# An encoder trunk on one core: how many weight quarters the first chunks hold, and in what order their first sums are made

## The chip, the cores and the metric

The kernel runs on one core of one Trainium2 chip. A core has five engines that work side by side, each on its own queue in program order: TensorE (PE, matrix products, with its weight loads shown apart as PEld), VectorE (DVE), ScalarE (ACT), GpSimd (POOL) and SyncE (SP, which here only issues transfers). The metric is the device time of one execution in microseconds (us), smaller being better. Three runs of the kernel before took 955.87, 958.1 and 958.0 us, so the median is 958.0 us.

## The reference

A two-layer encoder trunk over 512 tokens of width 1024. Each layer normalises the tokens, projects them with one wide matrix, mixes them (layer 0 by dilated sliding-window attention, layer 1 by grouped-query attention with a rotary over a grid), lets four memory heads look at 256 memory tokens, gates the heads, and projects the result back onto the residual.

```python
for i in range(DEPTH):
    h = rmsnorm(x, norm_g[i])
    mem_h = rmsnorm(mem, mem_norm_g[i])
    if i % 2 == 0:
        proj = jnp.einsum('bsd,de->bse', h, w_in_a[j])
        ...
        o_mix = mixer_dilated(qkv, qn_a[j], kn_a[j], ang_a)
    else:
        proj = jnp.einsum('bsd,de->bse', h, w_in_b[j])
        ...
    o_mem = memory_attention(q_mem, mem_h, w_mem_kv[i], mem_qn_g[i], mem_kn_g[i])
    y = jnp.concatenate([o_mix, o_mem], axis=-1) * jax.nn.silu(gate)
    x = x + jnp.einsum('bse,ed->bsd', y, w_out[i])
```

All of it is in 32-bit floats. The memory attention normalises the keys of each head (`k = rmsnorm(kv[:, :, 0], kn_g)`) before they meet the queries.

## The kernel before, in words

**Products.** Every number is kept as a high part (rounded to the matrix engine's 32-bit format) and a low part (what the rounding left). A product is made of three: high by high (line 173), low activation by high weight (174), high activation by low weight (177). ACT makes the high part of a weight tile (`wh`, line 309) and DVE the low part (`wo`, line 319).

**Seven products in place of eight.** A wide projection is cut into quarters, and the classic scheme of seven block products is used: the activations are needed as the quarters 12, 11, 22 and the sums S1, S2, S3, S4, the weights as the quarters 21, 11, 22 and the sums T1, T2, T3, T4. The order of the products is 12, 11, S1, S2, S4, S3, 22 with the weights 21, 11, T1, T2, 22, T3, T4.

**Chunks and groups.** The weights are read in chunks. In the order of work these are chunk 1 and 2 (keys and values of the memory, four groups each), chunk 0 (a value projection, two tiles of each weight, so fourteen groups), chunk 3 (memory queries, seven groups), chunk 4 (the first head, fourteen groups), and so on. A group is the set of matrix products made with one or two weight tiles. Groups are counted from 0 here: chunk 1 is groups 0 to 3, chunk 2 is 4 to 7, chunk 0 is 8 to 21, chunk 3 is 22 to 28.

**What orders the work.** The order is written by a small planner when the program is made. After every group it calls `advance`, which in this order writes low parts, at most one weight sum, up to two high parts, and then loads (`dma`, line 260, on the SP queue). Then it steps a counter of slots: slot n comes behind group n-1. Routines that are waiting for their slot (`spawn` with a delay, `yield n`) go on then. Work put in with `late` stands at the end of a slot, with `soon` at the start of the next. All engines keep this order; they wait for each other only for data and for room.

**Weight sums.** T1 is made by DVE (line 278). T2 (line 283), T3 (288) and T4 (293) are made by transfers issued on the POOL queue that add one tile, or a tile in DRAM, onto another. T2 needs T1, and T4 needs T2 and the low part of 21. A sum is only looked at when its load is two groups old, and T1 of the kernel before not ahead of group 8 (`T1_AT`).

**Loads.** `KEEP` is the number of weight tiles that may be loaded and not used up at a time, by the kind of chunk: 8 for chunks 1 and 2, 10 for chunk 0, 9 for chunks 3 and 4. The tiles (512 KB, name `wl`) share 23 buffers with the input rows and the activations. Stores of results (line 1062, `v0d`) and the small loads of `setup` (lines 975 to 978) stand in the same SP queue.

**The tokens.** Four blocks of 128 tokens are normalised one slot after the other from slot 2 on (`prep`): `norm_1` squares and sums on ACT, `norm_2` scales on DVE (line 495), `first_t` turns blocks 0 and 1 with the matrix engine, giving the quarters 12 and 11. `diffs_t` turns blocks 2 and 3 and makes S1 and S3 on DVE (561, 562), with a high and a low part for S1 (161, 164). `rest_t` makes S2 and S4 (573, 575) and the parts of S2, S4, S3 and 22 (569, 570), two slots between them.

**Memory keys.** `mem_kv` normalises the keys, turns them on the matrix engine (line 606, into a PSUM tile), writes the high part on ACT (643) and the low part on DVE (646). The turned keys and the turned tokens (name `xT`, line 501) take their PSUM tiles from the same four banks (`at`), the products (`pj`) from four others. The planner hands out, of the free banks, the one that has been free longest, and a bank is free when the last instruction that reads its tile has been written into the order.

Of the kernel before, what the change touches and what calls it, by code (L numbers as in the profile page):

```python
# [21 lines left out]
TCKW = {}  # L22
NBIG, NM4, NS2, SCRATCH = 7, 23, 14, 2048
RING, LEAD = 4, 2
BULK, ACTIVE, SET_AT, T1_AT, MEM_B, PREP_Y, PREP_B, HALF, SET_B = 2, 2, 15, 8, 14, 1, 1, {"a": 3, "b": 3, "o": 0}, 9
MEM_STEP = 1, 1
MEM_D = 4
DIRECT, DIRECT_B = (7,), (4, 5, 6, 7)
LO_K, LO_V = (0, 5), (0, 3)
PD = 2  # L30
EO = 2, 2, 1, 2, 2, 1
YB = {"m": (2, 2), "k": (1, 1, 1), 0: (1, 2, 1), 1: (1, 2, 1)}
# [6 lines left out]
SEQ = [1, 2, 0] + list(range(3, len(PLAN)))  # L39
T4_AT = {4: 4}  # L40
T1_DMA = 17
KEEP = {"T2": 8, "T2b": 6, "O1": 6, "W1": 9, "W2": 10, "W2s": 9, "W1bs": 9, "W1b": 7, "W2b": 9}


# [84 lines left out]
def trunk_kernel(ctx: ExitStack, tc: tile.TileContext, x, mem, wall, norm_g, mem_norm_g, gcol,  # L129
# [9 lines left out]
    drv = Driver()  # L139
# [4 lines left out]
    def m4(dt=F32, name="m4"):  # L144
        return pool.tile([128, 1024], dt, tag="m4", name=name, bufs=NM4)

    def s2(dt=F32, name="s2"):
        return pool.tile([128, 512], dt, tag="s2", name=name, bufs=NS2)
# [7 lines left out]
    def sm(n, name):  # L156
        return small.tile([128, n], F32, tag="sm%d" % n, name=name)
# [35 lines left out]
    class Weights:  # L193
        def __init__(self):
            self.items, self.last, self.need, self.allocs, self.sums = [], [], [], [], []
            self.users, self.kinds = {}, []
            g = 0
            for c in SEQ:
                kind, d = PLAN[c], sum(pieces(k) for k in PLAN[:c])
                base = len(self.items)  # L200
                if kind in GROUPS:
# [20 lines left out]
                else:  # L222
# [3 lines left out]
                    for k in ORDER:  # L226
                        for x in range(n):
# [5 lines left out]
                            if k != "T4":  # L233
                                self.users[c, k, x] = 1 if k in ("22", "T3") or k == "11" and c >= T1_DMA else 2
                            g += 1
                self.kinds += [kind] * (g - len(self.kinds))
            assert sum(pieces(k) for k in PLAN) == wall.shape[0]
            self.g = -1
            self.live = 0
# [9 lines left out]
                self.live -= 1  # L249

        def dma(self, most=9):
            while self.allocs and self.live < KEEP[self.allocs[0][2]] and most:
                most -= 1
                key, d, _ = self.allocs.pop(0)
                self.live += 1
                self.tile[key] = m4(name="wl")
                self.load_at[key] = self.g
                if key[1][0] != "T":
                    self.at[key] = self.g
                nc.sync.dma_start(self.tile[key], wall[d])  # L260
# [4 lines left out]
        def sum(self, force=False, want=None):  # L265

            for n, (key, d) in enumerate(self.sums[:8]):
                if want and key != want:
                    continue
                c, k, x = key  # L270
                if k == "T1" and c >= T1_DMA:
                    if not self.ripe(self.load_at, key, force):
                        continue
                    G.dma_start(self.tile[key], wall[d], accum_op=ALU.add)
                elif k == "T1":
                    if not (self.ripe(self.load_at, key, force) and self.ripe(self.at, (c, "11", x), force)) or self.g < T1_AT and not force:
                        continue
                    V.tensor_tensor(self.tile[key], self.tile[key], self.tile[c, "11", x], ALU.add)
                    self.use((c, "11", x))
                elif k == "T2":  # L280
                    if not (self.ripe(self.load_at, key, force) and self.ripe(self.at, (c, "T1", x), force, 1 if c < T1_DMA else None)):
                        continue
                    G.dma_start(self.tile[key], self.tile[c, "T1", x], accum_op=ALU.add)  # L283
                    self.use((c, "T1", x))
                elif k == "T3":
                    if not self.ripe(self.load_at, key, force):
                        continue
                    G.dma_start(self.tile[key], wall[d], accum_op=ALU.add)
                else:
                    if not (self.ripe(self.lo_at, (c, "21", x), force, 1) and self.ripe(self.at, (c, "T2", x), force, T4_AT.get(c))):  # L290
                        continue
                    self.tile[key] = self.tile[c, "21", x]
                    G.dma_start(self.tile[key], self.tile[c, "T2", x], accum_op=ALU.add)  # L293
                    self.use((c, "T2", x))
                self.at[key] = self.g
                self.sums.pop(n)
                return True
            return False

        def hi(self, force=False):  # L300
            i = self.n_hi
            if i >= len(self.items) or not self.ripe(self.at, self.items[i], force, 1 if self.items[i][1] == "T1" and self.items[i][0] < T1_DMA else None):
                return False
# [140 lines left out]
    def rstd_of(ss, n):  # L444

        r = sm(n, "rstd")
        e = sm(n, "mse")
        G.tensor_scalar(e, ss, EPS, None, ALU.add)  # L448
        G.tensor_tensor(r, e, half[:, 0:n], ALU.pow)  # L449
        return r  # L450
# [29 lines left out]
    def norm_1(xb, both=False):  # L480

        ss = sm(2, "ss")
        for j in range(2):
            jk = s2(name="sq")
            if both and j:
                V.tensor_tensor_reduce(jk, xb[j], xb[j], 1.0 / 1024.0, 0.0, ALU.mult, ALU.add, ss[:, j:j + 1])
            else:
                A.activation(jk, xb[j], AF.Square, scale=1.0 / 32.0, accum_out=ss[:, j:j + 1])
        r, e = sm(1, "rstd"), sm(1, "mse")
        G.tensor_tensor(e, ss[:, 0:1], ss[:, 1:2], ALU.add)  # L490
        return rstd_of(e, 1)

    def norm_2(xb, r, row, js=(0, 1)):
        for j in js:
            V.scalar_tensor_tensor(xb[j], xb[j], r, row[j], ALU.mult, ALU.mult)
# [44 lines left out]
    def slot(H, k, c):  # L540
        if c == 0:
            part[k] = big(F32R, "h" + k).rearrange("p (a k t) -> p a k t", a=2, k=4)
        else:
            H[k] = part[k]
        cs = slice(c * 128, (c + 1) * 128)
        return part[k][:, 0, :, cs], part[k][:, 1, :, cs]

    def first_t(H, top, c):

        ps = [(k, turn4(top[j], *slot(H, k, c))) for k, j in (("12", 1), ("11", 0))]  # L550
        for k, p in ps:
            A.copy(whole(k, c), p)

    def diffs_t(H, low, c):

        f22 = whole("22", c)
        A.copy(f22, turn4(low[1], None, None))
        p = turn4(low[0], None, None)
        yield 1
        s1, s3 = whole("S1", c), whole("S3", c)  # L560
        V.tensor_tensor(s1, p, f22, ALU.subtract)
        V.tensor_tensor(s3, full["11", c], p, ALU.subtract)
        split(*slot(H, "S1", c), s1)

    def rest_t(H, c, ds, spread=False):

        def put(k, f):
            hi, lo = slot(H, k, c)
            A.copy(hi, f)
            drv.late(lambda: V.tensor_tensor(lo, f, hi.bitcast(F32), ALU.subtract))  # L570

        s1, s2_, s4, s3, f22 = [full.pop((k, c)) for k in ("S1", "11", "12", "S3", "22")]
        V.tensor_tensor(s2_, s1, s2_, ALU.subtract)
        if not spread:
            V.tensor_tensor(s4, s4, s2_, ALU.add)
        put("S2", s2_)
        if spread:
            yield ds[0] - 1
            V.tensor_tensor(s4, s4, s2_, ALU.add)
            yield 1  # L580
        else:
            yield ds[0]
        put("S4", s4)
        yield ds[1]
        put("S3", s3)
        yield ds[2]
        put("22", f22)
        yield 1
# [24 lines left out]
    def halves(t):  # L613
        return [t[:, 0:512], t[:, 512:1024]]
# [339 lines left out]
    H, H2 = {}, {}  # L954
    xb = [halves(t) for t in xt]

    def prep():

        n = {}
        for c in range(5):  # L960
            if c < 4:
                n[c] = norm_1(xb[c])
            if c:
                norm_2(xb[c - 1], n[c - 1], rows["x"])
            if 1 < c < 4:
                first_t(H, xb[c - 2], c - 2)
            yield 1
        for c in range(2):
            yield from diffs_t(H, xb[2 + c], c)
            drv.spawn(rest_t(H, c, (2, 2, 2)), 1)  # L970
            yield 1

    def setup():

# [68 lines left out]
    def ahead(u, b):  # L1043
# [5 lines left out]
        if (u, b) == (0, 1):  # L1049
            place_m(0, 1)  # L1050
            place_m(1, 1)

    drv.spawn(prep(), PD)
    drv.spawn(setup(), SET_AT)

# [605 lines left out]
```

## Time and profile before

One execution was profiled. It took 955.29 us, of which 953.4 us lie between its first and last instruction (the span).

| | before |
|---|---|
| median of three runs | 958.0 us |
| profiled execution / its span | 955.29 / 953.4 us |
| PE busy | 939.3 us |
| DVE busy | 790.3 us |
| ACT busy | 680.8 us |
| POOL busy | 336.0 us |
| weight tiles loaded on the SP queue | 222 of 512 KB |

The profile gives, for each engine, busy time, the idle time ahead of an instruction and the one that ended it; the chain of waits that ends with the last instruction; and the timeline of each queue. Times in a timeline are counted from the start of the span. In a row of the timeline the columns are the start, the time from the first start to the last end, the engine, the line of the code, the operation, the tile that is written and those that are read, the shape, the number of instructions put together, and in brackets the idle time before them with what ended it. SPq is the SP queue's issuing of transfers.

### The profile page before, as it was taken

To read this page: it belongs to the slowest core of one execution; us is meant where nothing else is said; L and a number is where in the kernel's file an instruction comes from. 1 tells how busy PE (TensorE), PEld (TensorE's weight loads), DVE (VectorE), ACT (ScalarE), POOL (GpSimd) and SP (SyncE) were. 2 spreads that over 40 slices of the span, in tenths; PEclk is the share of its full clock that TensorE was granted. 3 is DMA by queue.
4 is the path that set the end of the run, shared out by engine and by line. 5 is a ranking of instruction groups with operands and counts; after the bars stand their busy time and mean duration, and the time that the engine had idled before them with its cause. 6 is when DMAs were issued, how large, how long until landed. Compare 5 with 4: busy or idle time off the path is not lost.

```text
span 953.4 us, 16569 instructions
## 1 busy us (share of the span) xinstructions
PE 939.3 (99%) x5680; PEld 832.2 (87%) x5680; DVE 790.3 (83%) x1409; ACT 680.8 (71%) x1700; POOL 336.0 (35%) x484
## 2 busy tenths in 40 slices
PE   8999999999999999999999999999899999999998
PEld 6878888888888888888889998888899999998886
DVE  6878776878888888979788999877988898779982
ACT  7773789686868686767775768547778877878860
POOL 3312423557454546463836111213232330111110
PEclk9999999999999999999999999999999999999999
DMA  9699966869787869696877989979966687786524
GB/s 352 271 217 337 335 156 177 289 123 265 148 259 157 264 155 265 155 257 142 229 182 197 259 200 252 288 251 314 240 158 132 192 236 174 210 210 178 123 59 129
DMA packets 86198, 203.51 MB, mean 213 GB/s; under 512 B 25057, under 2 KB 34529, under 8 KB 86114
## 3 DMA queue, kind: packets, MB, share of 16 engines
q1 hardware_dynamic: 66962, 139.46, 42.8%
q0 software_dynamic: 17856, 60.83, 34.4%
q10 hardware_dynamic: 1296, 2.16, 0.6%
q8 instruction: 45, 0.74, 0.3%
q14 instruction: 39, 0.32, 0.1%
HBM read 156.48 MB, written 11.34 MB: 176 GB/s over the span
## 4 chain that ended last, share of the span: by engine, by line
PE 84%; DMA 6%; DVE 5%; ACT 3%; issue 1%; SPq 1%; POOL 0%; DVEq 0%; POOLq 0%; ACTq 0%
PE pj L173 22%; PE pj L174 22%; PE pj L177 22%; PE qT L606 2%; DMA wl<-in_wall_dram 2%; DMA wl<-wl 2%; DVE wo L319 2%; PE sa L1181 1%; PE oo L1289 1%; PE pt L1268 1%; PE ptb L1491 1%; PE sa L1177 1%; DMA x<-in_x_dram 1%; DMA row<-in_norm_g_dram 1%; PE ob L177 1%
## 5 line engine op out<-in xcount | busy, mean ns | idle before, releaser
L319 DVE TENSOR_TENSOR wo<-wl,wh 128x1024 fp32r<-128x1024 f32 x255 | 312.3, 1231 | 5.3 <-ACT wh L309 5.1
L309 ACT CAST wh<-wl 128x1024 fp32r<-128x1024 f32 x255 | 268.5, 1060 | 42.9 <-PE pj L174 18.9
L173 PE MATMUL pj<-wh,hS 128*128 128x512 f32 (+1 forms) x448 | 158.0, 366 | 4.5 <-ACT sn L384 3.7
L174 PE MATMUL pj<-wh,hS 128*128 128x512 f32 (+1 forms) x448 | 152.6, 354 | 0.6 <-DVE hS L570 0.6
L173 PE MATMUL pj<-wh,h 128*128 128x512 f32 (+1 forms) x336 | 118.0, 365 | 0.3 <-DVE sn L401 0.3
L174 PE MATMUL pj<-wh,h 128*128 128x512 f32 (+1 forms) x336 | 114.2, 353 | 1.1 <-DVE h L570 1.1
L449 POOL TENSOR_TENSOR rstd<-mse,half 128x4 f32<-128x4 f32 (+2 forms) x96 | 101.7, 1059 | 8.0
L177 PE MATMUL pj<-wo,hS 128*128 128x512 f32 (+1 forms) x448 | 100.7, 354 | 0.0
L173 PEld LDWEIGHTS pj<-wh,hS 128*128 128x128 f32 x448 | 85.1, 190 | 15.4 <-ACT sn L384 4.3
L174 PEld LDWEIGHTS pj<-wh,hS 128*128 128x128 f32 x448 | 85.2, 190 | 11.1 <-DVE hS L570 0.8
L177 PEld LDWEIGHTS pj<-wo,hS 128*128 128x128 f32 x448 | 75.3, 191 | 12.0
L448 POOL TENSOR_SCALAR mse<-hss 128x4 f32<-128x4 f32 (+1 forms) x86 | 41.2, 479 | 117.6 <-ACT junk L594 113.2
L594 ACT ACTIVATE junk<-sn 128x128 f32<-128x128 f32 x264 | 79.1, 308 | 1.3 <-DVE sn L395 1.2
L1125 POOL TENSOR_TENSOR ta<-sn,tabs 128x128 f32<-128x128 f32 (+1 forms) x64 | 37.6, 595 | 117.8 <-DVE sn L599 91.2
L384 ACT COPY sn<-pj 128x512 f32<-128x512 f32 x116 | 64.5, 590 | 17.4 <-PE pj L177 16.6
L177 PE MATMUL pj<-wo,h 128*128 128x512 f32 (+1 forms) x336 | 74.9, 352 | 0.0
L174 PEld LDWEIGHTS pj<-wh,h 128*128 128x128 f32 x336 | 63.7, 190 | 8.8 <-DVE h L570 1.3
L173 PEld LDWEIGHTS pj<-wh,h 128*128 128x128 f32 x336 | 63.6, 189 | 8.0 <-DVE sn L401 0.7
L293 POOL DMA_DIRECT2D wl<-wl x33 | 30.3, 918 | 109.1 <-DVE wo L319 59.8
L401 DVE TENSOR_TENSOR sn<-pj,sn 128x512 f32<-128x512 f32 x87 | 59.5, 685 | 7.7 <-PE pj L177 7.3
L177 PEld LDWEIGHTS pj<-wo,h 128*128 128x128 f32 x336 | 56.0, 189 | 8.8
L283 POOL DMA_DIRECT2D wl<-wl x33 | 31.3, 974 | 77.8 <-DVE grA L984 19.3
(250 smaller groups left out, 2365.2 us busy)
## 6 DMA issues: line engine op xcount, KB each, us to landing
wl<-in_wall_dram SPq DMA_DIRECT2D x222, 512.0 KB, 7.4
wl<-wl POOLq DMA_DIRECT2D x66, 512.0 KB, 5.4
wl<-in_wall_dram POOLq DMA_DIRECT2D x42, 512.0 KB, 8.9
od<-o SPq DMA_DIRECT2D x11, 256.0 KB, 5.5
og<-od SPq DMA_DIRECT2D x10, 256.0 KB, 8.2
x<-in_x_dram SPq DMA_DIRECT2D x4, 512.0 KB, 9.0
v0d<-sn SPq DMA_DIRECT2D x8, 256.0 KB, 10.2
acc<-in_x_dram POOLq DMA_DIRECT2D x8, 256.0 KB, 7.3
```

Source lines behind the costliest of these rows:

```text
L173: T.matmul(o, a, b, start=start, stop=False, skip_group_check=True)
L174: T.matmul(o, c, d, start=False, stop=False, skip_group_check=True)
L177: T.matmul(o, a, b, start=False, stop=stop, skip_group_check=True)
L283: G.dma_start(self.tile[key], self.tile[c, "T1", x], accum_op=ALU.add)
L309: A.copy(wh, self.tile[self.items[i]])
L319: V.tensor_tensor(wo, self.tile[key], wh.bitcast(F32), ALU.subtract)
L384: A.copy(t, b)
L401: V.tensor_tensor(t, b, t, ALU.subtract if q == "12" else ALU.add)
L448: G.tensor_scalar(e, ss, EPS, None, ALU.add)
L449: G.tensor_tensor(r, e, half[:, 0:n], ALU.pow)
L594: A.activation(jk, p[:, j * 128:(j + 1) * 128], AF.Square, scale=by, accum_out=ss[:, j:j + 1])
L1125: G.tensor_tensor(ta[:, 0:n], xn[:, 0:n, 0:32], ropeA[:, 0, b, s0:s0 + n], ALU.mult)
```

## The change

Five things are changed, all of them for the first chunks.

1. Chunk 0 and chunk 3 may hold 14 weight tiles, chunk 4 may hold 12 (`KEEP_C`).
2. The first sums T1 of chunk 0 may start with group 7 in place of 8, the third sums T3 of chunk 0 not ahead of group 10; a sum of chunk 0 that is too early now ends the search (`break`) where T1 was passed over before.
3. The low parts of the memory keys in layer 0 stand nine slots later (`LO_K`).
4. `diffs_t` of the second half block stands one slot earlier, next to that of the first, and both stand in front of `rest_t` of the first, which stands one slot later.
5. Of block 2's two squares in `norm_1`, the second goes from ACT to DVE.

```diff
-BULK, ACTIVE, SET_AT, T1_AT, MEM_B, PREP_Y, PREP_B, HALF, SET_B = 2, 2, 15, 8, 14, 1, 1, {"a": 3, "b": 3, "o": 0}, 9
+BULK, ACTIVE, SET_AT, MEM_B, PREP_Y, PREP_B, HALF, SET_B = 2, 2, 15, 14, 1, 1, {"a": 3, "b": 3, "o": 0}, 9
...
-LO_K, LO_V = (0, 5), (0, 3)
+LO_K, LO_V = (9, 5), (0, 3)
...
+SUM_AT = {"T1": 7, "T3": 10}
+KEEP_C = {0: 14, 3: 14, 4: 12}
...
-            while self.allocs and self.live < KEEP[self.allocs[0][2]] and most:
+            while self.allocs and self.live < KEEP_C.get(self.allocs[0][0][0], KEEP[self.allocs[0][2]]) and most:
...
                 c, k, x = key
+                if not c and not force and self.g < SUM_AT.get(k, 0):
+                    break
...
-                    if not (self.ripe(self.load_at, key, force) and self.ripe(self.at, (c, "11", x), force)) or self.g < T1_AT and not force:
+                    if not (self.ripe(self.load_at, key, force) and self.ripe(self.at, (c, "11", x), force)):
                         continue
...
-                n[c] = norm_1(xb[c])
+                n[c] = norm_1(xb[c], c == 2)
...
-        for c in range(2):
+
+        def forms(c):
             yield from diffs_t(H, xb[2 + c], c)
-            drv.spawn(rest_t(H, c, (2, 2, 2)), 1)
-            yield 1
+            yield 2
+            yield from rest_t(H, c, (2, 2, 2))
+
+        drv.spawn(forms(1), 1)
+        yield from forms(0)
```

## The prediction

> **What bounds the kernel now.** I read the page first, then the waits of the matrix engine, then its timeline, then the other queues in the stretch where it waits.
>
> ```profile
> PE 939.3 (99%) x5680; PEld 832.2 (87%) x5680; DVE 790.3 (83%) x1409; ACT 680.8 (71%) x1700; POOL 336.0 (35%) x484
> PE 84%; DMA 6%; DVE 5%; ACT 3%; issue 1%; SPq 1%; POOL 0%; DVEq 0%; POOLq 0%; ACTq 0%
> ```
>
> PE is busy 99% of the span and carries 84% of the chain. The change takes no product away, so it can only win back time in which PE waits or runs slowly. The longest entry in the list of PE's waits (who waited for whom: us in total, times, longest) lies in the first hundred microseconds:
>
> ```profile
> PE pj L173 <- ACT sn L384: 3.7, 2, 1.9
> ```
>
> PE's timeline shows these two, and a small one between them:
>
> ```profile
> 48.00 1.07 PE L177 MATMUL pj<-wo,h 128*128 128x512 f32 x4
> 50.97 0.50 PE L173 MATMUL pj<-wh,hS 128*128 128x512 f32 x1 [1.90 <-ACT sn L384]
> ...
> 55.04 0.63 PE L173 MATMUL pj<-wh,hS 128*128 128x512 f32 x1
> ...
> 57.23 1.07 PE L177 MATMUL pj<-wo,hS 128*128 128x512 f32 x4
> 58.14 0.39 PE L173 MATMUL pj<-wh,hS 128*128 128x512 f32 x1
> ...
> 60.86 0.39 PE L173 MATMUL pj<-wh,hS 128*128 128x512 f32 x1
> ...
> 75.14 0.39 PE L174 MATMUL pj<-wh,h 128*128 128x512 f32 x1
> 75.80 0.50 PE L173 MATMUL pj<-wh,h 128*128 128x512 f32 x1 [0.27 <-DVE sn L401]
> ...
> 93.94 1.12 PE L177 MATMUL pj<-wo,hS 128*128 128x256 f32 x8
> 96.83 0.38 PE L173 MATMUL pj<-wh,hS 128*128 128x256 f32 x1 [1.78 <-ACT sn L384]
> ```
>
> Starts tell more than the modelled ends. Four L177 products take 0.91 us (57.23 to 58.14), so group 11 is done at 48.91 and group 12 starts 2.06 us late. A full group takes 2.72 us (58.14 to 60.86), but group 12 takes 4.07 (50.97 to 55.04) and group 13 takes 3.10: 1.73 us more than two full groups. At 75.37 (75.14 and one product of 0.23) PE loses 0.43 us. At 94.90 (93.94 and 0.96 for eight products) it loses 1.93 us. The slow groups are the granted clock (columns: stretch, length, busy of PE, PEld, DVE, ACT, POOL, clock, DMA share, GB/s):
>
> ```profile
> 53.00:54.00 1.00, 1.00 (x4) 0.81 (x3) 1.00 (x2) 1.00 (x2) 0.06 (x1) 0.50 1.08 127
> ...
> 97.00:98.00 1.00, 1.00 (x9) 1.00 (x10) 0.86 (x1) 1.00 (x2) 1.00 (x1) 1.00 1.00 410
> ```
>
> The clock was halved after the wait of 2.06 us and not after that of 1.93. All that is to be won here is 2.06 + 1.73 + 0.43 + 1.93 = 6.15 us.
>
> **Part 1, more quarters live: the wait at 94.90.** The chain back from there, and the SP queue:
>
> ```profile
> 66.01 9.13 DMA wl<-in_wall_dram
> 75.67 9.34 DMA wl<-wl
> 85.60 8.41 DMA wl<-wl
> 94.09 1.05 ACT wh L309
> ```
>
> ```profile
> 16.18 15.81 SPq L260 DMA_DIRECT2D wl<-in_wall_dram  x13
> 56.58 2.06 SPq L1062 DMA_DIRECT2D v0d<-sn  x2
> 66.01 6.33 SPq L260 DMA_DIRECT2D wl<-in_wall_dram  x6
> ```
>
> The load of 66.01 is chunk 3's tile for T2. It brings the sum T2 at 75.67, that brings T4 at 85.60, and ACT stands before T4's high part until 94.09, with the copy that PE needs behind it. It is late since SP, done with thirteen loads at 32.0, stood before the first two value stores until 56.58 and then had other loads and the four of setup to issue. With limits of 14, chunk 0's last tiles are written into the order in group 2 and chunk 3's six in groups 4 to 11, all ahead of those stores (slot 14). Thus five loads move past the stores and past setup. SP issues a load about every 1.2 us (15.81 for thirteen), so they leave by about 32.0 + 5 x 1.2 = 38. No row shows chunk 3's T2 bound by anything then but its T1, which DVE makes with group 15 in place of 16. T4 still needs the low part of 21, written with group 20 (the group of 75.80, done some 2 us behind that), and 8.41 us behind 78 is 86: some 8 us before ACT was let go at 94.09. I take the whole 1.93 us off; the other end is 0, if another operation of ACT is late there. DVE's T1 of chunk 3 no longer waits for its load, so the 0.43 us at 75.37, a DVE add that was late, goes too (other end 0). Chunk 4's loads come three tiles further forward by group 19. They are hidden behind products either way and I cost them at nothing; without that cover one load is 1.2 us.
>
> **Parts 2 to 5, the wait at 48.91.** DVE's queue decides there. These rows are its timeline, then PE's and ACT's:
>
> ```profile
> 26.00 1.29 DVE L164 TENSOR_TENSOR h<-xT,h 128x512 fp32r<-128x512 f32 x2 [1.67 <-ACT h L161]
> ...
> 38.05 0.74 DVE L646 SCALAR_TENSOR_TENSOR kmT<-qT,gc,kmT 128x512 fp32r<-128x512 f32 x1
> 38.71 0.68 DVE L561 TENSOR_TENSOR fS<-xT,f 128x512 f32<-128x512 f32 x1
> 39.30 0.68 DVE L562 TENSOR_TENSOR fS<-f,xT 128x512 f32<-128x512 f32 x1
> ...
> 44.18 1.22 DVE L278 TENSOR_TENSOR wl<-wl 128x1024 f32<-128x1024 f32 x1
> 45.31 0.75 DVE L646 SCALAR_TENSOR_TENSOR kmT<-qT,gc,kmT 128x512 fp32r<-128x512 f32 x1
> 45.97 0.68 DVE L573 TENSOR_TENSOR f<-fS,f 128x512 f32<-128x512 f32 x1
> ...
> 47.96 1.22 DVE L278 TENSOR_TENSOR wl<-wl 128x1024 f32<-128x1024 f32 x1
> ...
> 50.46 0.69 DVE L164 TENSOR_TENSOR hS<-fS,hS 128x512 fp32r<-128x512 f32 x1
> ```
>
> ```profile
> 36.64 0.60 PE L606 MATMUL qT<-ident,xn 128*128 128x128 f32 x4
> 36.99 0.48 PE L173 MATMUL pj<-wh,h 128*128 128x512 f32 x1
> ...
> 39.85 1.03 PE L501 MATMUL xT<-ident,x 128*128 128x128 f32 x8
> 40.65 0.48 PE L173 MATMUL pj<-wh,h 128*128 128x512 f32 x1
> ```
>
> ```profile
> 24.77 0.63 ACT L488 ACTIVATE sq<-x 128x512 f32<-128x512 f32 x1
> ```
>
> ```profile
> L1187 DVE CUSTOM_DVE_ANT_0 p<-sa,tabs 128x256 f32<-128x256 f32 x48 | 19.0, 421 | 1.2 <-PE sa L1177 1.0
> L1187 DVE CUSTOM_DVE_ANT_0 p<-sa,tabs 128x192 f32<-128x192 f32 x16 | 5.7, 353 | 0.2 <-PE sa L1177 0.2
> ```
>
> The square that goes to DVE: no such row of 512 exists here. The two rows of its kind grow by 68 ns for 64 elements, so 421 + 4 x 68 = 0.69 us is my estimate. It lies in DVE's idle 1.67 us ahead of 26.00, so it costs nothing; without that cover, 0.69. ACT loses 0.63 us there, and DVE, which waits for ACT, starts up to that much sooner. I take 0.6 us (ends 0 and 0.63).
>
> Before S1 and S3 of the first half (561, 562), one key low part is gone (38.05 to 38.71, 0.66 us) and one T1 sum is new (1.13 us, 44.18 to 45.31). So line 562 ends at 39.98 - 0.66 + 1.13 - 0.6 = 39.85 (39.82 to 40.45).
>
> Now the price of moving things forward. The two turned key tiles keep their PSUM banks until their low parts are written, nine slots later. Of four `at` banks two remain. In slot 8, behind group 7, PE must turn the two tiles of the second half; the first gets the free bank, the second the bank that line 562 of the first half still reads. PE gets there at 36.64 + 0.35 (turned keys, 36.64 to 36.99) + 0.40 (half of 39.85 to 40.65) = 37.39 and waits to 39.85: **a new wait of 2.46 us** (2.43 to 3.06), with the products of group 8 queued behind it. In the kernel before the same tile took a bank that the low part of 38.05 had left, one slot later, and the row at 39.85 shows no wait. The eight transposes themselves only change place.
>
> Then group 12 could start at 48.91 + 2.46 = 51.37. Does it still wait there? S1's last low part ended at 51.15; in front of it 1.99 us of S2 and S4 (45.97 to 47.96) go behind, 1.32 of key low parts go, 0.6 is gained: 47.2, or a microsecond later with DVE's wait for ACT. The two copies that free the banks of group 12 stand behind S2's first high part on ACT, by my estimate until about 49.6. So no wait is left at group 12, and it starts 51.37 - 50.97 = 0.40 us later than before. The two key low parts fall in slots 17 and 18, where nothing needs them before the memory attention. The third sums come in group 11 and 12, directly behind the second ones on POOL as before: nothing.
>
> The halved clock: does it follow a wait of 2.46 us at 37.39? The nearest row, 2.06 us, was followed by it, so I keep its 1.73 us (ends 0 and 1.73).
>
> The page "TensorE: Matmul & The Clock Gate" of the Trainium skill (Part 1) says that the clock falls to half after an idle window of about 3.4 us, in windows that run on freely. By that no wait of 2.46 us could fill a window and the sum would be 1.73 us lower; this trace differs, since the clock was at 0.50 after 2.06 us.
>
> **The sum.** 955.29 + 0.40 + 1.73 - 1.73 - 0.43 - 1.93 = 953.3 us against the profiled execution. That stands 2.7 us under the median of 958.0. In a run of 958 the wait of 1.93 us may well have had its own halved clock; this would go with it. So of the 2.7 I give back 2.7 - 1.73 = 1.0: **954.3 us**.
>
> **The rivals.**
> - *No halved clock behind the new wait.* For it: 1.93 us had none. Against: 2.06 had. 954.3 - 1.73 = 952.6.
> - *No bank wait.* The second half's tile finds a free bank, or DVE is there sooner. For it: nothing in the rows, only that the order is worked out by hand. Then group 12 starts at 49.6 with the copies, 1.4 us sooner than before: 954.3 - 1.73 - 0.40 - 1.4 = 950.8.
> - *A new lock of DVE.* POOL's two rope products stood at 78.92 behind chunk 3's late third sum; now they start with setup's DVE work of slot 19, one group ahead of group 20 and so at about 71. One DVE subtraction beside them took 4416 ns in place of 685:
>
> ```profile
> 78.92 3.99 POOL L987 TENSOR_TENSOR tabs<-tabA,grA 128x768 f32<-128x768 f32 x2
> L395 DVE TENSOR_TENSOR sn<-sn x29: 677/685/4416, 79.1 to 873.8; 128x512 f32<-128x512 f32 x29
> ```
>
>   Those 3.7 us were hidden at 79; eight microseconds sooner the add that frees group 20's bank is behind them. With about 2.5 us of them on PE the time is 956.8, no measurable change.
> - *Slower: T2 of chunk 0 comes late.* Its transfer now starts behind T1 at about 39 (39.85 less two subtractions), while SP's last loads are landing. It decides if it lands after 57 (group 14's 58.14 less 1.05 for the high part); each microsecond later costs one. With 18 us from issue to landing nothing is lost; at 26 us it is 8 us, 962. Against it: 9.34 us was the longest of these chain rows.
>
> **How the numbers follow.** Forecast 0.42 (954.3, its own range 953 to 956), no halved clock 0.16, no bank wait 0.10, the lock 0.20, late T2 0.12. A measurement of this kernel tells about 0.3% from no change, 2.9 us: faster is under 955.1, slower over 960.9. Faster: three quarters of the forecast (0.32) and both better cases, 0.58. Same: the rest of the forecast and the lock, 0.30. Slower: 0.12. The range goes from 950.3 (no bank wait) to 959.0 (the lock in full, 3.7 us and 1 of scatter), which leaves out the late T2.
>
> **What would show it.** PE's timeline should show transposes (line 501) waiting for line 562 near 37.4 us, no wait at group 12, a clock of 0.50 for some 3.4 us around 40, and no wait of PE for the copy of line 384 near 95. On SP eighteen loads in place of thirteen should leave ahead of the first value store, the last by about 40. The prediction is wrong if PE waits elsewhere before 100, if DVE is held beside line 987, or if anything behind 100 differs by more than the shift.

## The result and the profile after

The changed kernel took 953.16 us (median of twelve runs, 952.24 to 955.39), the kernel before 956.15 us beside it (twelve runs, 955.35 to 959.87). The ratio is 0.9964, with a 95% interval of 0.9954 to 0.9974: faster by 0.36%. The profiled execution took 953.29 us with a span of 951.4 us, against 955.29 and 953.4 before. 954.3 us had been predicted, and 953.3 for a profiled execution.

In the changed kernel's code line numbers behind 41 are two to eight higher: 173, 174, 177 of before are 175, 176, 179; 260 is 262; 278, 283, 293 are 282, 287, 297; 319 is 323; 384 and 401 are 388 and 405; 501 is 505; 561 and 562 are 565 and 566; 606 is 610; 646 is 650; 987 is 995.

Two lines of the page of the kernel after (busy time of each engine; shares of the chain):

```profile
PE 937.2 (99%) x5680; PEld 830.7 (87%) x5680; DVE 790.0 (83%) x1411; ACT 681.1 (72%) x1698; POOL 340.0 (36%) x484
PE 90%; DVE 4%; ACT 2%; DMA 2%; issue 1%; POOL 0%; SPq 0%; DVEq 0%; ACTq 0%; POOLq 0%
```

PE carries 90% of the chain in place of 84%. Its timeline in the first hundred microseconds:

```profile
36.43 0.60 PE L610 MATMUL qT<-ident,xn 128*128 128x128 f32 x4
36.87 0.60 PE L505 MATMUL xT<-ident,x 128*128 128x128 f32 x4
39.78 0.63 PE L505 MATMUL xT<-ident,x 128*128 128x128 f32 x4 [2.32 <-DVE fS L566]
...
51.15 0.39 PE L175 MATMUL pj<-wh,hS 128*128 128x512 f32 x1
...
53.87 0.39 PE L175 MATMUL pj<-wh,hS 128*128 128x512 f32 x1
...
56.59 0.39 PE L175 MATMUL pj<-wh,hS 128*128 128x512 f32 x1
...
73.81 0.39 PE L175 MATMUL pj<-wh,h 128*128 128x512 f32 x1
...
86.02 1.12 PE L179 MATMUL pj<-wo,hS 128*128 128x256 f32 x8
88.08 0.38 PE L175 MATMUL pj<-wh,hS 128*128 128x256 f32 x1 [0.94 <-DVE sn L405]
...
96.81 0.60 PE L1099 MATMUL qT<-ident,sn 128*128 128x128 f32 x4
```

and the row of before that answers to the last of them:

```profile
99.80 0.38 PE L1091 MATMUL qT<-ident,sn 128*128 128x128 f32 x2
```

Read by starts, as in the prediction: the second tile of the second half block could have started at 36.87 + 0.40 = 37.27 and starts at 39.78, so PE loses 2.51 us there. Group 12 starts at 51.15 (before 50.97), without a wait. Groups 12 and 13 take 2.72 us each, so the clock was not halved, and group 14 starts 1.55 us ahead of before (56.59 against 58.14). The fifth product of group 20 starts 1.99 us ahead (73.81 against 75.80): the small wait at 75.37 is gone. The products of 86.02 end at 86.98 and the next starts at 88.08, which is a new wait of 1.10 us. The row of 96.81 stands 2.99 us ahead of its twin: the wait at 94.90 is gone.

Here are the other queues: SP, then POOL, then DVE, of the kernel after.

```profile
16.49 21.64 SPq L262 DMA_DIRECT2D wl<-in_wall_dram  x18
54.99 2.04 SPq L1070 DMA_DIRECT2D v0d<-sn  x2
```

```profile
63.57 0.86 POOL L287 DMA_DIRECT2D wl<-wl  x1 [9.44 <-issue]
...
70.17 4.69 POOL L995 TENSOR_TENSOR tabs<-tabA,grA 128x768 f32<-128x768 f32 x2 [4.82 <-DVE grA L992]
76.30 0.90 POOL L297 DMA_DIRECT2D wl<-wl  x1 [1.45 <-DVE wo L323]
```

```profile
37.23 1.22 DVE L282 TENSOR_TENSOR wl<-wl 128x1024 f32<-128x1024 f32 x1
38.36 0.68 DVE L565 TENSOR_TENSOR fS<-xT,f 128x512 f32<-128x512 f32 x1
38.96 0.68 DVE L566 TENSOR_TENSOR fS<-f,xT 128x512 f32<-128x512 f32 x1
...
42.05 2.35 DVE L323 TENSOR_TENSOR wo<-wl,wh 128x1024 fp32r<-128x1024 f32 x2
...
46.83 0.69 DVE L166 TENSOR_TENSOR hS<-fS,hS 128x512 fp32r<-128x512 f32 x1
...
70.60 5.34 DVE L323 TENSOR_TENSOR wo<-wl,wh 128x1024 fp32r<-128x1024 f32 x2
79.25 1.23 DVE L282 TENSOR_TENSOR wl<-wl 128x1024 f32<-128x1024 f32 x1 [3.31 <-DMA wl<-in_wall_dram]
```

Eighteen loads leave ahead of the first value store, the last by 38.13. Chunk 3's T2 is issued at 63.57 (before 75.67) and its T4 at 76.30 (before 85.60). Line 566 ends at 39.64. New is the last row: DVE stands for 3.31 us in front of chunk 4's first sum, whose load has not landed. What PE needs at 88.08, a sum of line 405, is queued behind it.

So PE is 2.99 us ahead at 96.81 and yet the span is only 2.0 us shorter. The chain of waits of the kernel after shows where 1.0 is given back; under it stand the chain of before at the same place and two rows of its SP queue:

```profile
848.68 7.24 DMA odb<-o
856.00 0.37 SPq L815
856.42 3.35 DMA og<-odb
859.79 0.69 DVE yf L829
```

```profile
860.01 1.14 DVE wo L319
861.17 1.29 DVE yf L825 x2
```

```profile
851.59 0.33 SPq L1381 DMA_DIRECT2D odb<-o  x1
...
857.67 0.89 SPq L811 DMA_DIRECT2D og<-odb  x2
```

A store to DRAM and the load that reads it back take 11.1 us from 848.68 to 859.79, and DVE and then PE wait for them. In the trace of before the store leaves at 851.59. The second of the two reloads leaves at about 858.1 and lands 3.0 us later, so the pair took some 9.5 us, and DVE, which comes to the product that needs it at 861.77 (the second of the row of 861.17), does not wait.

### The profile page after: what moved, and what is told of

Its sections match the earlier page's. It is cut to its first block, busy times and chain, and to the rows that moved or that the text cites. A ratio compares the mean times of both kernels' runs of the same rounds, so it can differ in the third digit from the quotient of the medians.

```text
span 951.4 us, 16573 instructions
## 1 busy us (share of the span) xinstructions
PE 937.2 (99%) x5680; PEld 830.7 (87%) x5680; DVE 790.0 (83%) x1411; ACT 681.1 (72%) x1698; POOL 340.0 (36%) x484
## 4 chain that ended last, share of the span: by engine, by line
PE 90%; DVE 4%; ACT 2%; DMA 2%; issue 1%; POOL 0%; SPq 0%; DVEq 0%; ACTq 0%; POOLq 0%
PE pj L176 24%; PE pj L175 24%; PE pj L179 24%; PE qT L610 2%; PE sa L1189 2%; PE oo L1297 2%; PE pt L1276 1%; PE ptb L1499 1%; DVE wo L323 1%; PE sa L1185 1%; PE ob L179 1%; DMA odb<-o 1%; PE pmt L735 1%; DMA m<-in_mem_dram 1%; PE ob L176 1%
## 5 line engine op out<-in xcount | busy, mean ns | idle before, releaser
L1133 POOL TENSOR_TENSOR ta<-sn,tabs 128x128 f32<-128x128 f32 (+1 forms) x64 | 39.8, 629 | 116.6 <-DVE sn L603 91.1
```

The lines of the kernel that those rows point to most:

```text
L1133: G.tensor_tensor(ta[:, 0:n], xn[:, 0:n, 0:32], ropeA[:, 0, b, s0:s0 + n], ALU.mult)
```

## The experiments

Every kernel was timed beside the kernel before, whose medians in the three sets were 957.11, 957.25 and 956.41 us. The table puts together what follows. The second column adds up the idle times in brackets between 36 and 140 us in PE's timeline of the profiled execution (0.2 us and more), the third tells whether a halved clock follows.

| kernel | PE's waits, us | clock halved | profiled, us | ratio to before (95%) |
|---|---|---|---|---|
| before | 1.90 + 0.27 + 1.78 | yes | 955.29 | 1 |
| all limits alone | 1.89 + 0.22 + 0.51 + 0.68 + 1.41 | no | 955.49 | 0.9992 (0.9983 to 1.0002) |
| limits of chunks 0 and 3 alone | 1.98 | yes | 953.13 | 0.9961 (0.9949 to 0.9974) |
| first sums from group 7 alone | 1.90 + 0.22 | no | 953.01 | 0.9958 (0.9946 to 0.9970) |
| the change | 2.32 + 0.94 | no | 953.29 | 0.9964 (0.9954 to 0.9974) |
| without the limits | 2.31 | yes | 953.89 | 0.9964 (0.9951 to 0.9978) |
| first sums from 8 | 1.34 + 0.71 + 0.68 + 1.40 | no | 953.71 | 0.9980 (0.9971 to 0.9990) |
| without limits, first sums from 8 | 1.19 + 0.57 + 1.00 | no | 953.83 | 0.9976 (0.9966 to 0.9986) |
| old order of the forms | 0.20 + 0.56 + 0.68 + 1.40 | no | 952.83 | 0.9964 (0.9950 to 0.9977) |
| keys' low parts at once | 1.71 + 1.07 | no | 952.81 | 0.9961 (0.9948 to 0.9973) |
| square on ACT | 2.93 + 0.49 | no | 952.98 | 0.9967 (0.9954 to 0.9979) |
| second turn one slot later | 0.54 + 0.68 + 1.41 | no | 952.55 | 0.9955 (0.9942 to 0.9968) |
| later turn, without the limits | none | no | 950.89 | 0.9934 (0.9922 to 0.9946) |
| later turn, chunk 4's first sum later | 0.49 | no | 950.07 | 0.9932 (0.9919 to 0.9945) |

**All limits alone.** The kernel before with the larger limits, first sums still from group 8, third sums from 10 (in this diff and in the like one below, the lines of the change that read these values, and those that drop `T1_AT`, are not shown).

```diff
+SUM_AT = {"T1": 8, "T3": 10}
+KEEP_C = {0: 14, 3: 14, 4: 12}
```

> The kernel before with the new limits of 14, 14 and 12 quarters, and with the third sums held until group 10 so that they do not come sooner with the loads; keys, forms, squares and the first sums as before. Theory (the loads in front of the stores alone take the later waits away): PE's waits of 0.43 us near 75 and 1.93 us near 95 are gone, the wait of 2.06 us at group 12 stays, a wait of about 0.9 us near 88 to 90 appears as in the changed kernel; about 1.5 us under the kernel before, 954.7 against 956.15. Rival (the wait near 95 hangs on DVE and ACT being late from group 12 on, not on the loads): the wait near 95 stays and the time is within 0.5 us of the kernel before.

956.34 us, no change that can be told, where 954.7 had been expected. The waits at 75 and 95 are gone, but others stand in their place. PE's timeline, then the row of DVE:

```profile
86.66 0.36 PE L175 MATMUL pj<-wh,hS 128*128 128x256 f32 x1 [0.68 <-DVE sn L405]
...
91.17 0.39 PE L175 MATMUL pj<-wh,hS 128*128 128x256 f32 x1 [1.41 <-DVE sn L405]
```

```profile
82.35 1.23 DVE L282 TENSOR_TENSOR wl<-wl 128x1024 f32<-128x1024 f32 x1 [5.42 <-DMA wl<-in_wall_dram]
```

This is the wait of the change at 88.08 in a larger form. The row of DVE is chunk 4's first sum. The limit of 12 lets its load be written into the order early, so the planner takes it for ripe two groups later and puts the sum into DVE's queue. On SP the load has value stores and setup's loads in front of it, and lands behind the sum's turn. DVE works in order and stands.

**The change without the limits.**

```diff
-KEEP_C = {0: 14, 3: 14, 4: 12}
+KEEP_C = {}
```

> The changed kernel with the old limits of quarters, all else changed. Theory: PE waits some 2.4 us for its PSUM bank near 37 and not at group 12, which starts within 0.4 us of 50.97; the wait of 1.93 us near 95 stays; within 0.8 us of the kernel before, 955.4 to 956.9. Rival (the order of the forms is what wins the time): group 12 starts at the same time but the wait near 95 is gone and the time is that of the changed kernel, 953.2.

953.89 us and the ratio of the change, where 955.4 to 956.9 had been expected: the limits add nothing to it. The wait at 95 stays away without them. PE, SP and POOL of this kernel:

```profile
40.35 0.98 PE L505 MATMUL xT<-ident,x 128*128 128x128 f32 x4 [2.31 <-DVE fS L566]
```

```profile
16.69 15.87 SPq L262 DMA_DIRECT2D wl<-in_wall_dram  x14
...
57.24 2.44 SPq L262 DMA_DIRECT2D wl<-in_wall_dram  x2
```

```profile
67.43 0.86 POOL L287 DMA_DIRECT2D wl<-wl  x1 [14.54 <-DVE wl L282]
```

A first sum made one group earlier uses up its tile of 11 one group earlier, so one load more fits: fourteen leave ahead of the stores in place of thirteen. The two behind the stores are then chunk 3's for T1 and T2, and both stand ahead of setup's four small loads. In the kernel before, T2's load was the next one, and stood behind them at 66.01. T2 goes out at 67.43 in place of 75.67, early enough.

**First sums from group 7 alone.** If that reading holds, one number in the kernel before must do it.

```diff
-BULK, ACTIVE, SET_AT, T1_AT, MEM_B, PREP_Y, PREP_B, HALF, SET_B = 2, 2, 15, 8, 14, 1, 1, {"a": 3, "b": 3, "o": 0}, 9
+BULK, ACTIVE, SET_AT, T1_AT, MEM_B, PREP_Y, PREP_B, HALF, SET_B = 2, 2, 15, 7, 14, 1, 1, {"a": 3, "b": 3, "o": 0}, 9
```

> The kernel before with one number changed: first sums T1 of chunk 0 from group 7 in place of 8. Theory: the quarter that the sum frees comes free a group sooner, so fourteen loads in place of thirteen leave ahead of the first value store, chunk 3's loads for T1 and T2 stand ahead of the four loads of setup, and the wait of 1.93 us at 94.90 (with the small one at 75.37) goes without any larger limit. The wait at group 12 (2.06 us at 48.91) stays or grows by up to 1.1 us, since a first sum more stands on DVE ahead of S1's low part, and whether the clock halves behind it is open. Time 954 to 955.5 us beside 956 to 957. Rival: the wait at 94.90 goes by the new order of the forms and the keys' low parts (they clear DVE and ACT), not by the loads; then it stays here at 1.5 us or more and the time is 956 to 958.

953.01 us, as fast as the whole change. Its PE and its SP queue:

```profile
51.35 0.50 PE L173 MATMUL pj<-wh,hS 128*128 128x512 f32 x1 [1.90 <-ACT sn L384]
...
56.39 1.21 PE L177 MATMUL pj<-wo,hS 128*128 128x512 f32 x4 [0.22 <-DVE wo L319]
```

```profile
16.37 16.37 SPq L260 DMA_DIRECT2D wl<-in_wall_dram  x14
```

The wait at group 12 is there as before, and there is none at 75 or 95. It came out some 1 us better than the expected range, which left the halved clock open: in the profiled execution the clock was not halved, and in four of the five runs its mean was 1.0.

**The limits of chunks 0 and 3 alone.** The same loads moved forward in the other way, with first sums from 8.

```diff
+SUM_AT = {"T1": 8, "T3": 10}
+KEEP_C = {0: 14, 3: 14}
```

> The kernel before with larger limits for chunks 0 and 3 alone (14 tiles each); chunk 4 keeps its limit of 9, first sums stay at group 8 and the forms and keys as before. Theory: what takes the wait at 94.90 away is that chunk 3's load for T2 leaves SP ahead of the value stores and setup's loads; the limits of chunks 0 and 3 do that (eighteen loads ahead of the first store). The limit of chunk 4 did the harm when all limits were raised alone: it brought chunk 4's first sum ahead of its load in DVE's order, with PE waits of 0.68 and 1.41 us at 86.66 and 91.17. Without it that sum stands where the kernel before has it, so PE has no wait between 60 and 140 except one of about 0.5 at 60, the wait of 1.9 to 2.1 us at group 12 stays, and the time is 953 to 954.5 us. Rival: the limits are worth nothing in themselves and only the earlier first sum clears the path; then waits of 1.5 us or more between 80 and 97 remain and the time is 955.5 to 957.

952.93 us; PE's only wait is the one at group 12, with the halved clock behind it (PE's timeline, then a stretch of one microsecond with the columns of the prediction's table):

```profile
51.46 0.50 PE L175 MATMUL pj<-wh,hS 128*128 128x512 f32 x1 [1.98 <-ACT sn L388]
```

```profile
53.00:54.00 1.00, 1.00 (x4) 0.81 (x3) 0.96 (x2) 0.94 (x3) 0.55 (x1) 0.50 1.33 188
```

The group 60 wait that was expected at about 0.5 did not come. Two unlike edits that bring chunk 3's loads forward take the same wait away, so it is the loads; and what spoils it in the set of all limits is chunk 4's alone (0.9992 against 0.9961, some 3 us).

**First sums from 8, with and without the limits.**

```diff
-SUM_AT = {"T1": 7, "T3": 10}
+SUM_AT = {"T1": 8, "T3": 10}
```

> The changed kernel with the first sums of chunk 0 from group 8 again in place of 7. Theory (the T1 sum stands in front of line 566 on DVE and lengthens the bank's wait by its 1.13 us): the wait near 37 is 1.3 us in place of 2.46, group 12 starts at about 50.0; about 1.1 us under the changed kernel, 952.1. Rival (the T1 sums are needed early, and what is won near 37 is lost again at group 12 or 13): 953.2.

The wait on the bank shrinks by 0.98 us, about one first sum of DVE (1.13 us), to 1.34. But the time is 954.93 us where 952.1 had been expected, and the ratio is 0.9980 against 0.9964 of the change. The two intervals just overlap, so that the kernel is slower is likely, not shown. The reason is in the trace: with a load less between stores and setup, chunk 4's first sum stands 4.73 us for its own, and PE waits for 2.79 us between 83 and 90.

```diff
-SUM_AT = {"T1": 7, "T3": 10}
-KEEP_C = {0: 14, 3: 14, 4: 12}
+SUM_AT = {"T1": 8, "T3": 10}
+KEEP_C = {}
```

> The changed kernel without the larger limits and with first sums T1 of chunk 0 from group 8, as before: the order of the forms, the keys' low parts, the third sums and the square on DVE alone. Theory: thirteen loads leave ahead of the first value store again, chunk 3's T2 load stands behind setup's, and the wait at about 95 returns with 1.5 to 2 us though the bank wait near 38 shrinks to about 1.3 us. Time 954.5 to 955.5 us, some 1 us over the changed kernel without the larger limits. Rival: the wait at 95 is taken away by the order of the forms; then it stays gone, and the time is 1 us under the changed kernel without the larger limits, 952 to 953.

The time is as expected, 954.55 us, the place is not. PE's rows, then POOL's:

```profile
72.32 1.19 PE L179 MATMUL pj<-wo,hS 128*128 128x512 f32 x4 [0.57 <-DVE wo L323]
...
75.83 0.50 PE L175 MATMUL pj<-wh,h 128*128 128x512 f32 x1 [1.00 <-DVE sn L405]
```

```profile
74.95 0.86 POOL L287 DMA_DIRECT2D wl<-wl  x1 [20.27 <-DVE gk L989]
```

T2 is as late as before (74.95), and chunk 3's late loads cost 1.73 us at 72 to 76 (with a wait of 0.16 between these rows) where they cost 0.43 and 1.93 before. At 95 nothing is left to wait for. Why the loss moves there wholly I have not tried further.

**The turn of the second half block one slot later.** This tests the bank.

```diff
-            yield 2
+            yield 2 if c else 3
...
-        drv.spawn(forms(1), 1)
+        drv.spawn(forms(1), 2)
```

> The changed kernel with the turning of the second half block one slot later (behind group 8 in place of group 7) and the sums S2 and S4 of both halves one slot later each; the order of DVE's sums is the same. Theory (PE waits near 37 only since the second tile gets the PSUM bank that line 566 of the first half still reads): no wait near 37, the transposes start at about 39.5, and group 12 starts at 48.6 to 49.2 in place of 51.15; about 2 us under the changed kernel, 951.1. Rival (DVE's work up to the low parts sets group 12 anyway, and the bank only shows it): PE waits at group 12 instead, which starts at 51 again; 953.2.

The wait near 37 is gone and group 12 starts at 49.08: the bank is confirmed. But of the 2.3 us some 1.7 are lost again at chunk 4's first sum (2.63 us of waits in place of 0.94). PE, then DVE:

```profile
82.02 1.21 PE L179 MATMUL pj<-wo,h 128*128 128x256 f32 x8 [0.54 <-DVE wo L323]
...
83.92 0.36 PE L175 MATMUL pj<-wh,hS 128*128 128x256 f32 x1 [0.68 <-DVE sn L405]
...
88.43 0.39 PE L175 MATMUL pj<-wh,hS 128*128 128x256 f32 x1 [1.41 <-DVE sn L405]
```

```profile
79.60 1.23 DVE L282 TENSOR_TENSOR wl<-wl 128x1024 f32<-128x1024 f32 x1 [3.53 <-DMA wl<-in_wall_dram]
```

The groups are 2 us earlier, the load lands when it did (79.25 before the edit, 79.60 with it), so PE meets the standing DVE more fully.

**The keys' low parts at once**, from the other side:

```diff
-LO_K, LO_V = (9, 5), (0, 3)
+LO_K, LO_V = (0, 5), (0, 3)
```

> The changed kernel with the low parts of the memory keys written at once, as before, and not nine slots later. Theory: the bank wait of 2.46 us at 37.39 comes from the two banks that the turned keys keep; with the first key tile's low part written ahead of line 565, its bank is free when the second half block is turned, so that wait goes, or shrinks to under 1 us. The two low parts stand in DVE's queue again ahead of S1's last low part (1.32 us later, about 48.2), which group 12 still does not wait for by more than 0.5. The waits between 82 and 90 grow to about 2.5 us as with the later turn. Time 952 to 953. Rival: the bank is still held by line 566 of the first half block; then the wait at 37 stays at 2.5 us or more (line 566 ends 0.66 later) and the time is 953.5 to 954.5.

```profile
39.54 0.66 PE L505 MATMUL xT<-ident,x 128*128 128x128 f32 x4 [1.71 <-DVE kmT L650]
```

In this row of PE the tile now waits for the low part of a key (line 650) and not for line 566: it takes the key's bank, as the theory has it. The wait shrinks to 1.71 us only, not to under 1, because the first sum of 1.13 us stands ahead of that low part on DVE too. The wait near 88, expected to grow to about 2.5 us, is 1.07. The time, 952.85 us, can't be told from the change's.

**The old order of the forms.**

```diff
-
-        def forms(c):
+        for c in range(2):
             yield from diffs_t(H, xb[2 + c], c)
-            yield 2
-            yield from rest_t(H, c, (2, 2, 2))
-
-        drv.spawn(forms(1), 1)
-        yield from forms(0)
+            drv.spawn(rest_t(H, c, (2, 2, 2)), 1)
+            yield 1
```

> The changed kernel with the old order of the forms: the second half block's S1 and S3 behind S2 and S4 of the first. Theory: no bank wait near 37, since the tile finds a bank that the first half block has left; but S1's last low part then stands behind S2 and S4 again, so the wait at group 12 returns with some 0.7 us (2.06 less 1.3 for the two key low parts that are gone from in front). With the groups up to 1.5 us earlier the waits of chunk 4's first sum between 82 and 90 grow from 0.94 to about 2.5 us. Time 952.5 to 954, the changed kernel within 1 us. Rival: the new order of the forms is what the gain comes from; then the wait at group 12 is back with 2 us, followed by a halved clock, and the time is 955 or more.

953.38 us and the change's ratio. There is no wait at 37 and none of 0.2 us at group 12, where 0.7 had been expected (0.20 us at 53.97 is all ahead of 82), so moving the two key parts and the square away was enough for group 12, and the new order of the forms, as placed, bought nothing: it paid 2.5 us for a bank to save a wait that was gone. The old order loses 2.64 us to chunk 4's first sum between 82 and 90. What it would do without that loss was not run.

**The square on ACT.**

```diff
-                n[c] = norm_1(xb[c], c == 2)
+                n[c] = norm_1(xb[c])
```

> The changed kernel with block 2's second square on ACT, as before. Theory: ACT makes the first high parts up to 0.63 us later, DVE follows, line 566 ends up to 0.6 us later than 39.64, and the bank wait grows from 2.46 to 2.5 to 3.1 us. Time: up to 0.6 us over the changed kernel, 953.2 to 954.0. Rival: DVE is not bound by ACT there and the move is worth nothing; then line 566 ends at 39.6 and the time is the changed kernel's within 0.2 us.

```profile
40.88 0.63 PE L505 MATMUL xT<-ident,x 128*128 128x128 f32 x4 [2.93 <-DVE fS L566]
```

The bank's wait grows from 2.32 to 2.93 us, 0.61 as expected. Line 566 ends 1.10 us later than in the change, at 40.74, but PE too reaches the second tile 0.48 us later in this trace (a row of transposes at 37.35 in place of 36.87), so the wait shows what the square is worth. The time, 953.82 us, is not told apart from the change's.

**Both waits taken away.** First without the limits, then with them and chunk 4's first sum held back until its load is four groups old.

```diff
-KEEP_C = {0: 14, 3: 14, 4: 12}
+KEEP_C = {}
...
-            yield 2
+            yield 2 if c else 3
...
-        drv.spawn(forms(1), 1)
+        drv.spawn(forms(1), 2)
```

> The changed kernel without the larger limits for chunks 0, 3 and 4, and with S1 and S3 of the second half block turned one slot later, so that their tile finds a bank that line 562's block has left. Theory: two separate things. The bank wait (2.46 us at 37.39 after the change) goes by the later turn, as it did when only the turn was moved; the waits of PE at 82 to 90 that then came (0.54, 0.68 and 1.41 us) stem from chunk 4's first sum, which the larger limits bring into DVE's order ahead of its load, so without the limits they do not come. PE then has no wait over 0.3 us between 36 and 140 except at most 0.5 where the turn stood, group 12 starts near 49.1 us, and no wait near 95, since the first sum of chunk 0 in group 7 still puts fourteen loads ahead of the stores. Time: the changed kernel's less 2.46 and less 0.94, about 950 to 951 us beside 956 to 957 of the kernel before. Rival: the waits at 82 to 90 come from the groups being earlier, not from the limits; then they stand here too (2 to 3 us) and the time is 952.5 to 953.5.

```diff
-                    if not (self.ripe(self.load_at, key, force) and self.ripe(self.at, (c, "11", x), force)):
+                    if not (self.ripe(self.load_at, key, force, 4 if c == 4 else None) and self.ripe(self.at, (c, "11", x), force)):
...
-            yield 2
+            yield 2 if c else 3
...
-        drv.spawn(forms(1), 1)
+        drv.spawn(forms(1), 2)
```

> The changed kernel with its larger limits kept, the second half block turned one slot later, and chunk 4's first sum T1 looked at only when its load is four groups old in place of two. Theory: DVE's 3.3 to 3.5 us of standing before that sum (its load lands near 79.5 us) is what makes PE wait between 82 and 90; with the sum behind its load in the order, DVE does not stand there and those waits (2.63 us with the turn alone moved) go. Time about 950 to 951 us, the turn alone moved less 1.5 to 2.6. Rival: DVE is held by POOL's rope products beside it (two low parts in 5.34 us in place of 2.36), not by the load; then the waits stay within 0.5 us and the time is 952 to 953.

950.89 and 950.38 us, ratios 0.9934 and 0.9932: both beat the change, whose interval begins at 0.9954, and can't be told from each other. The first has no wait of PE of 0.2 us or more between 36 and 140, the second one of 0.49 us, behind a DVE row that had stood 4.67 us for a small operation on POOL (PE's row first, then two of DVE). In the second DVE is still held beside POOL's rope products, by the same 3.0 us (three low parts in 6.48 us, in 3.51 elsewhere; in the change two in 5.34 and 2.35), and PE does not wait for it:

```profile
102.99 0.65 PE L1099 MATMUL qT<-ident,sn 128*128 128x128 f32 x4 [0.49 <-DVE sn L603]
```

```profile
70.52 6.48 DVE L323 TENSOR_TENSOR wo<-wl,wh 128x1024 fp32r<-128x1024 f32 x3
...
84.47 3.51 DVE L323 TENSOR_TENSOR wo<-wl,wh 128x1024 fp32r<-128x1024 f32 x3
```

So the lock was not what made PE wait between 82 and 90; the sum ahead of its load was. With the later turn and the old age of two groups, the limits seem to cost some 2 us (0.9955 with them, 0.9934 without, with intervals that just overlap).

## Why the prediction was right, and which steps were wrong

The time came within 0.2% and inside the range, and the profiled execution met its sum of 953.3 us to 0.1 us. That agreement is partly luck: the terms differ and cancel. The prediction had +0.40, +1.73, -1.73, -0.43 and -1.93, together -1.96. The trace has +0.18 at group 12, -1.73 for the clock, -0.44 by group 20, -1.93, +1.10 and a -0.17 that I can't assign between there and 96.81, and +1.0 at 860: together -2.0. The last step, 1.0 us on top for the median of 958.0, did not hold: that was a median of three runs, and over twelve runs it is 956.15 us, so the profiled execution lay 0.9 us under it and not 2.7. It accounts for nearly all of the 1.1 us between 954.3 and 953.16.

- **The bank wait: right, in place, cause and size.** 2.46 us at 37.39 was worked out, 2.51 at 37.27 came, behind line 566 (39.85 predicted, 39.64 measured). The later turn took it away, and the keys' tiles are the holders.
- **Group 12: right.** It no longer waits; S1's last low part ended at 47.5 where 47.2 to 48.2 was said. But the old order of the forms has no wait there either, so of the reasons given (S2 and S4 put behind, two key parts gone, the square moved) the order was not needed.
- **The square's 0.6 us: right**, 0.61.
- **Part 1, "I take the whole 1.93 us off": right in mechanism and size, wrong in who pays.** Chunk 3's late T2 load was the cause, and the limits of chunks 0 and 3 alone take both waits away. What the prediction missed is that part 2, the first sums one group earlier, does the same by itself, since it frees a tile. It was priced as 1.13 us of DVE time and nothing else. In the change the gain is there twice and counts once.
- **"Chunk 4's loads come three tiles further forward ... I cost them at nothing": wrong.** A load moved forward in the planner's order also moves the sum that waits for it. The sum came ahead of its load's landing and held DVE for 3.31 us; PE paid 1.10 in the change and 2.1 to 2.8 in four other kernels. This is the step that kept the change from being worth more.
- **The halved clock "stays": did not show in the profile.** In the fourteen profiled executions the mean granted clock was 0.998 in the three with a halved clock and 0.999 or 1.0 in the others. In the change's twelve runs it was 0.998 in six and 0.999 or 1.0 in six; their mean times are 953.8 and 952.8 us. By that sign the forecast and its rival without a halved clock each came in about half of the runs, but no trace shows the clock halved behind the wait at 37 in the change, and the difference is 1.0 us and not the 1.73 of the sum.
- **The lock of DVE: it came, at 70.60 as said (5.34 us for two low parts, 2.35 without it), but cost nothing**: behind it DVE had to stand for a load in any case, and in the kernel where it did not, PE still had no wait. The late T2 of chunk 0 did not come: no wait of PE between 40 and 86.
- **"If anything behind 100 differs by more than the shift": it did,** by 1.0 us at 860. The store and reload there took some 9.5 us in one trace and 11.1 in another, without any edit near them. DVE stood for the reload 0.83 us in the change, 1.02 with first sums from 7 alone, 0.27 and 0.34 in two other kernels and next to nothing in the rest. With one trace of each kernel it is not shown whether this is scatter or follows from the shift in time; a sum made for one profiled execution carries it either way.

The Trainium skill's page "TensorE: Matmul & The Clock Gate" (Part 1) says that its activity windows run on freely, and that an idle window of about 3.4 us halves the clock. The first half fits the table: in it halving followed waits of 1.90, 1.98 and 2.31 us and did not follow 1.89, 1.90, 2.32 and 2.93, so length alone doesn't decide. The second half does not fit, as none of these waits was 3.4 us long.

The Trainium skill's page "SBUF — State Buffer" (section "SBUF: two separate sides") says that VectorE and GpSimd share a pair of ports under an exclusive lock, taken also by a VectorE operation with two inputs in SBUF. The trace agrees: two such low parts took 5.34 us beside POOL's products of 70.17 to 74.86, and 2.35 at other places.

## What to carry to other kernels

A planner that counts a load as ripe by groups since it was written into the order knows nothing of what stands ahead of it in the queue. When limits are raised, look for the in-order engine that now meets the operation before its data, and hold that operation back or let its load go first. And when several parts of a change clear the same late load, try each alone before pricing them as a sum: here one number gave all that the change gave (0.9958), and the rest, put right by one slot and one age, took the ratio to 0.9932, some 2.5 us more.

## What was not expected of the hardware

Whether the clock is halved behind a wait of about 2 us differed from kernel to kernel and run to run. The kernel before had a mean clock of 0.998 or less in 44 of its 49 runs over the three sets, though the other five were no more than 0.3 us faster in the mean (956.4 against 956.7 for the 37 at 0.998). In the change without limits the same difference was 2.6 us (954.0 in five runs, 951.5 in two). A reason would be that in the kernel before PE's lost time was partly waited for anyway at 95, where the transfers decide; that is not shown.
